# Serial steps of a recurrence wait for the next unit's tiled matmuls and share their groups

## Chip, cores and metric

One core of a Trainium2 chip runs the whole program. The metric is device time in microseconds (us), the median of several runs; lower is better. The engines are TensorE (PE, with PEld for its weight loads), VectorE (DVE), ScalarE (ACT), GpSimd (POOL) and SyncE (SP), which issues the DMA transfers.

## The reference

A decoder trunk of two layers, 512 positions, model width 1024, all in float32. Each layer projects its input x with one wide matrix into four gated branches of width 512, and merges them:

```
for l in range(2):
    h = x @ w_in[l]                      # split among the branches
    y_rwkv = rwkv7(...)                  # branch 0
    y_mla  = latent_attention(...)       # branch 1
    y_conv = conformer_conv(...)         # branch 2
    y_mem  = cross_attention(...)        # branch 3
    proj   = einsum('bsnc,ncd->bsnd', stack(y_rwkv, y_mla, y_conv, y_mem), w_o_branch[l])
    merged = sum(sigmoid(merge + b_gate[l]) * proj, over n)
    x = layer_norm(alpha * x + merged @ w_out[l])
```

The branch that the change touches is a recurrence over the positions, for 8 heads with a state of 64 x 64 each:

```
def step(state, inp):
    r_t, w_t, k_t, v_t, a_t, b_t = inp
    sa = einsum('bhvk,bhk->bhv', state, a_t)
    state = state * w_t + sa[..., None] * b_t + v_t[..., None] * k_t
    return state, einsum('bhvk,bhk->bhv', state, r_t)
y = group_norm(y) * lnx_g + lnx_b + bonus, then times silu(gate)
```

## The kernel before

**One stream and side tasks.** The large projections are matmuls of 128x128 weights by 512 columns, each product made of three (high by low, high by high, low by high parts), called from `mm3` through `MM` (L286). They form one stream in a fixed order (`stream`). Everything else (attention blocks, convolution, the recurrence) is written as Python generators, "tasks". A planner (`Plan`) decides once, while the program is built, where a task's next piece goes between pieces of the stream. It keeps its own clock per engine; a task that yields a function sleeps until it is true, one that yields "slack" waits for the planner's DVE clock, one that yields "small" has a piece of tiled 64x64 matmuls. The planner holds "small" pieces back (for up to `GATHER`) unless TensorE has just been switched to another tile shape, so that pieces that are due together come together. On the chip nothing of that is left but an order of instructions per engine and semaphore waits between engines.

**The recurrence in units.** `rwkv_unit` handles two channel blocks (four heads) over 256 positions: four units in each layer, `un` = 0 to 3, where units 1 and 3 go on from the state of 0 and 2. A unit works on four chunks of 64 positions with matrices of 64x64, as tiled matmuls of which four fit TensorE side by side. Its pieces are, by the names of the tiles that they write: zw (decay and rate), D (powers of the decay with a first column of ones), g (products of keys and receptances), M and Mc (the triangular part and its 16x16 diagonal blocks), a substitution on POOL that inverts those blocks (Mc goes out to a scratch tensor and comes back as W; the result comes back as zc, tc and zq, over SP's queue), bo and tk (full matmuls and transposes), x0, x1, x2 (the inverse is put together by blocks), va, gb (which gives Gs, H, B and Y0), then the **serial steps** w0 to w3: one after the other the state is multiplied by Gs (two tiled matmuls of 64x64 for each of two channel blocks) and S = w * D + H is formed on DVE. yb then applies the states to B, Y0 is added, eight bn_stats and bn_aggr and POOL's gr give the norm, ACT applies it to yb, ty transposes it and DVE adds it into r.

**What sets the order.** The units overlap: a unit starts when `L["mids"] == un` (the unit ahead has formed Gs, H, B, Y0). Its x0 waits until its substitution is back and `L["chains"] == un`, that is until the unit ahead has done all its serial steps and yb. The serial steps yield "small" and run as soon as the planner can place them. Tiles of a unit are in a pool (`rk`) by tags; tiles of one tag share a buffer, and T, Q, Z and PT are taken over by Gs, H, B and Y0. D has two buffers of its own, `dpads`, whose first column is set once at the start.

**After the last unit.** When `L["units"]` is 4 the recurrence's pool is closed, and the phase that ends the layer opens in the same memory: in layer 1 SP issues 16 loads of z and 8 of ln_g and ln_b, then the weights w220 and on. Weight loads have two buffers, so the load of w219 waits until the splits of w217 into high and low parts (ACT, then DVE) are done. ps_rg, ps_m and po are the gate, merge and output projections around that place.

Of the kernel before, what the change touches and what calls it, by code (L numbers as in the profile page):

```python
# [265 lines left out]
def trunk_kernel(ctx: ExitStack, tc: tile.TileContext, A, out, dbg=None):  # L266
# [4 lines left out]
    def MM(o, lhsT, rhs, start, stop, four=False):  # L271
        n = 1
        for d in rhs.shape[1:]:
            n *= d
        k, m = lhsT.shape[0], lhsT.shape[-1]
        plan.shape(64 if k <= 64 else 128, 64 if m <= 64 else 128)
        if max(k, m) <= 64:
            c = max(0.42 * n + 1.0, 29.0) if four else max(0.83 * n + 12.0, 59.0)
        elif rhs.dtype != F32 or n < 16:
            c = max(0.4167 * n + 13.0, 109.0) * (2 if rhs.dtype == F32 else 1)  # L280
        elif m <= 64:
            c = 0.83 * n + 3.0
        else:
            c = 1.667 * n + 5.0
        plan.op("PE", c, _names(o), _names(lhsT, rhs))
        plan.keep(nc.tensor.matmul(o, lhsT, rhs, start=start, stop=stop))  # L286

    def TR(o, i):
        plan.shape(128, 128)
        plan.op("PE", 109.0, _names(o), _names(i))  # L290
        plan.keep(nc.tensor.transpose(o, i, ident))  # L291
# [65 lines left out]
    for t in hpads:  # L357
        G.memset(t[:, 0:30], 0.0)
    dpads = [cp.tile([128, 8, 65], F32, tag=f"dpad{i}", name=f"dpad{i}") for i in range(2)]
    for t in dpads:  # L360
        G.memset(t[:, :, 0:1], 1.0)

# [235 lines left out]
    def layer_items(l):  # L598
# [97 lines left out]
        L["yr"] = [None] * 4  # L696
        L["units"] = L["chains"] = L["mids"] = L["subs"] = L["read"] = 0

# [13 lines left out]
        def chunks(ap):  # L712

            return ap.rearrange("p (a b) w -> p b a w", b=2)

        def by2(ap):
            return ap.rearrange("p (a b) w -> p a b w", a=2)

        def both(ap):

            return ap.rearrange("p s (c w) -> p (s c) w", w=64)

        def rwkv_unit(j0, hf, rkv):
# [8 lines left out]
            def rk(tag, shape, name=None, dt=F32, bufs=1):  # L732
                return L["rp"].tile([128] + shape, dt, tag=tag, name=(name or tag) + t, bufs=bufs)
# [19 lines left out]
            yield  # L753
            D = dpads[un % 2]
            S.activation(D[:, :, 1:65], both(cum), AF.Exp, scale=-1.0)
            E = rk("s0", [2, 256], "E")
            S.activation(E, cum, AF.Exp)
# [35 lines left out]
            V.reciprocal(rn[:, :, 1:4:2], s1[:, :, ::-1, 1])  # L793
            M = rk("M", [2, 4, 64])
            gm = g0[:, :, 0:256].rearrange("p h (s c w) -> p s h c w", s=2, c=2)
# [4 lines left out]
            M8 = M.rearrange("p s c w -> p (s c) w")  # L800
            Mc = rk("Mc", [8, 16])
            V.tensor_scalar(out=Mc, in0=M8[:, :, 0:16], scalar1=bm[:, 0:1], scalar2=None, op0=ALU.mult)
# [101 lines left out]

            yield lambda: L["subs"] > un and L["chains"] == un
            zc, tc_, zq = zt
# [8 lines left out]
            yield  # L915

            x0, y0 = yield from pg.take([128, 2, 512], "x0" + t, 2, "small")
            x0, y0 = (x.rearrange("p c (q s a w) -> p q s c a w", q=2, s=2, a=2) for x in (x0, y0))
# [52 lines left out]
            for s in SUB:  # L971
                for cp, c2, h in quads:
                    MM(x2[HALF[h ^ cp], 1, s, c2, h], NQ[s][HALF[c2], 2 * h + cp, 0], vt[s][HALF[c2], 2 * h + cp], start=True, stop=True, four=True)
            yield
            Z = rk("Z", [2, 4, 64], "Zi")
# [15 lines left out]
            pg.free()  # L991
            yield
            gbs = yield from pg.take([128, 2, 512], "gb" + t, 2, "small")
            gb, hh, y0 = ([x[:, :, a:b].rearrange("p c (a w) -> p c a w", a=2) for x in gbs] for a, b in ((0, 256), (256, 384), (384, 512)))
# [17 lines left out]
            yield  # L1012
            Gs, H, B, Y0 = (rk(tag, [2, 4, 64], n) for tag, n in (("T", "Gs"), ("Q", "H"), ("Z", "B"), ("PT", "Y0")))
            for s in SUB:
                V.tensor_tensor(out=by2(H[:, s]), in0=hh[s], in1=chunks(D[:, 4 * s:4 * s + 4, 64:65]).to_broadcast([128, 2, 2, 64]), op=ALU.mult)
                V.tensor_tensor(out=by2(Gs[:, s]), in0=gb[s][:, :, :, 0:64], in1=cc("id2")[:, 0:64].unsqueeze(1).unsqueeze(1).to_broadcast([128, 2, 2, 64]), op=ALU.add)
                S.copy(by2(Y0[:, s]), y0[s])
# [3 lines left out]
            L["mids"] += 1  # L1021
            yield


            states = [[zero, zero] if hf == 0 else [state[j] for s, j in js]]
            for c in range(4):
                e = 2 * (c % 2) + c // 2
                if hf == 0 and c == 0:
                    states.append([H[:, s, 0] for s in SUB])
                elif hf == 0 or c < 3:  # L1030
                    ps, = yield from pa.take([128, 2, 64], f"w{c}" + t, 1, "small")
                    for s in SUB:
                        for half in HALF:
                            MM(ps[half, s], Gs[half, s, e], states[c][s][half], start=True, stop=True)
                    yield
                    s1 = rk("S", [2, 64], f"S{c}", bufs=6)
                    for s in SUB:
                        V.scalar_tensor_tensor(out=s1[:, s], in0=ps[:, s], scalar=D[:, 4 * s + c, 64:65], in1=H[:, s, e], op0=ALU.mult, op1=ALU.add)
                    pa.free()
                    states.append([s1[:, s] for s in SUB])  # L1040
                    yield
            for s, j in js:
                state[j] = states[-1][s]
            ps, = yield from pg.take([128, 2, 512], "yb" + t, 1, "small")
            yp = ps[:, :, 0:256].rearrange("p h (s a w) -> p s h a w", s=2, a=2)
# [3 lines left out]
            yield  # L1049
            yb = rk("yb", [2, 4, 64])  # L1050
            for s in SUB:
# [8 lines left out]
            for e in range(8):  # L1060
                if e % 2 == 0:
                    yield "slack"
                V.bn_stats(bs[:, 6 * e:6 * e + 6], y8[:, e])
            yield "slack"
            for e in range(8):
# [12 lines left out]
            for a in range(4):  # L1078
                TR(ps[:, 128 * a:128 * a + 128], y8[:, 2 * a:2 * a + 2].rearrange("p e w -> p (e w)"))
            yield  # L1080
            for s, j in js:
                yield "slack"
                for a in range(2):
                    src = ps[:, 256 * s + 128 * a:256 * s + 128 * a + 128].rearrange("p (c w) -> p c w", c=2)
                    o = rr[s].rearrange("p (b a w) -> p b a w", b=2, a=2)[:, :, a]
                    if a:
                        src = src[:, ::-1]
                    V.scalar_tensor_tensor(out=o, in0=src, scalar=pr("lnx_g", j), in1=o, op0=ALU.mult, op1=ALU.add)
# [933 lines left out]
```

## Time and profile before

| | before |
|---|---|
| median of 3 runs | 1519.35 us (1518.24 to 1521.86) |
| span of the profiled execution | 1518.1 us |
| first matmul / last matmul's end in it | 6.1 us / 1508 us |
| TensorE busy | 1485.7 us |
| DVE, ACT, POOL busy | 1072.7, 686.6, 135.8 us |

How to read it: the span runs from the first to the last instruction of one execution. "Busy" counts from an instruction's start to its modelled end, and matmuls are pipelined, so the ends overlap the next starts; for TensorE the distance between starts says more than the duration. In a timeline row stand the start, the duration, engine, line, operation, the tiles written and read, the tile shape of the array (128*128 is full, 64*64 is tiled), the operand's size, and how many alike were merged in the row; in brackets the idle time before it and what ended it. A tiled float32 matmul shows as two records. In rows of groups stand the durations in ns (minimum, median, maximum).

### The profile page before, as it was taken

To read this page: it belongs to the slowest core of one execution; us is meant where nothing else is said; L and a number is where in the kernel's file an instruction comes from. 1 tells how busy PE (TensorE), PEld (TensorE's weight loads), DVE (VectorE), ACT (ScalarE), POOL (GpSimd) and SP (SyncE) were. 2 spreads that over 40 slices of the span, in tenths; PEclk is the share of its full clock that TensorE was granted. 3 is DMA by queue.
4 is the path that set the end of the run, shared out by engine and by line. 5 is a ranking of instruction groups with operands and counts; after the bars stand their busy time and mean duration, and the time that the engine had idled before them with its cause. 6 is when DMAs were issued, how large, how long until landed. Compare 5 with 4: busy or idle time off the path is not lost.

```text
span 1518.1 us, 29700 instructions
## 1 busy us (share of the span) xinstructions
PE 1485.7 (98%) x11896; PEld 1238.0 (82%) x11896; DVE 1072.7 (71%) x2231; ACT 686.6 (45%) x1499; POOL 135.8 (9%) x323
## 2 busy tenths in 40 slices
PE   8999999999999999999999999999999999999997
PEld 8877788887887878888999877888887878788886
DVE  5788988765757675555554889997766586756747
ACT  5535653445245453344255556533443545443432
POOL 0000000030402021000010000000030303120002
PEclk9999999999999999999999999999999999999999
DMA  6443333322232323433343252433232323235231
GB/s 211 124 113 93 104 100 98 98 85 83 74 93 60 94 74 93 139 98 114 123 146 114 81 125 69 121 107 97 81 99 61 93 64 93 69 95 181 98 116 65
DMA packets 89018, 153.54 MB, mean 101 GB/s; under 512 B 41008, under 2 KB 47152, under 8 KB 88880
## 3 DMA queue, kind: packets, MB, share of 16 engines
q1 hardware_dynamic: 88880, 151.65, 33.9%
q8 instruction: 93, 1.52, 0.4%
q14 instruction: 45, 0.37, 0.1%
HBM read 134.32 MB, written 5.77 MB: 92 GB/s over the span
## 4 chain that ended last, share of the span: by engine, by line
PE 89%; DVE 5%; DMA 2%; ACT 2%; issue 1%; SPq 1%; POOL 0%; ACTq 0%; DVEq 0%; POOLq 0%
PE ps_m L286 22%; PE po L286 11%; PE ps_cg L286 3%; PE ps_rg L286 3%; PE ps_v L286 3%; PE ps_xg L286 3%; PE ps_mg L286 3%; PE ps_k L286 3%; PE ps_r L286 3%; PE ps_val L286 3%; PE pz L286 2%; PE ms L286 2%; PE pl L286 2%; PE ps_glu L286 2%; PE ps_xq L286 2%; PE x L286 2%
## 5 line engine op out<-in xcount | busy, mean ns | idle before, releaser
L235 DVE SCALAR_TENSOR_TENSOR cacc<-hpad,prm,cacc 128x512 f32<-128x512 f32 x240 | 178.9, 748 | 3.3
L235 ACT ACTIVATE tm<-ps_m,prm 128x512 f32<-128x512 f32 x64 | 44.1, 689 | 148.5 <-PE ps_m L286 134.7
L235 DVE SCALAR_TENSOR_TENSOR mt<-tm,po 128x512 f32<-128x512 f32 x48 | 33.0, 687 | 79.2 <-PE po L286 79.1
L235 POOL TENSOR_SCALAR ZT<-W 64x256 f32<-64x256 f32 x8 | 4.8, 600 | 621.8 <-DMA W<-scr 287.7
L235 POOL TENSOR_TENSOR ZT<-ZT,tmpW 64x14 f32<-64x14 f32 (+6 forms) x112 | 44.0, 393 | 8.8
L235 ACT ACTIVATE mP<-ms,nmm 128x512 f32<-128x512 f32 (+3 forms) x64 | 33.7, 529 | 18.3 <-DVE nmm L235 17.4
L235 POOL TENSOR_TENSOR tmpW<-ZT,W 64x14 f32<-64x14 f32 (+6 forms) x112 | 39.9, 356 | 7.9
L235 ACT COPY mPT<-mt 128x512 f32<-128x512 f32 (+3 forms) x64 | 26.7, 429 | 22.4 <-PE mt L291 17.1
L235 DVE TENSOR_TENSOR merged<-merged,mt 128x512 f32<-128x512 f32 x48 | 33.8, 704 | 1.6
L235 DVE TENSOR_REDUCE nmm<-ms 128x1 f32<-128x512 f32 (+3 forms) x64 | 29.9, 483 | 0.6 <-PE ms L286 0.2
L235 POOL TENSOR_SCALAR gr<-gm 128x8 f32<-128x8 f32 x8 | 2.3, 286 | 311.2 <-DVE gm L235 311.2
L291 PE MATMUL mt<-cst,mP 128*128 128x128 f32 x160 | 27.1, 276 | 2.6 <-DVE mP L235 2.2
L235 DVE SCALAR_TENSOR_TENSOR merged<-tm,po 128x512 f32<-128x512 f32 x16 | 11.0, 687 | 22.0 <-PE po L286 20.3
L235 DVE TENSOR_SCALAR mP<-mP,smm 128x512 f32<-128x512 f32 (+3 forms) x64 | 24.8, 387 | 2.3
L235 ACT ACTIVATE yb<-yb,mr,gr 128x64 f32<-128x64 f32 x64 | 22.1, 430 | 9.0 <-DVE mr L235 9.0
L235 POOL TENSOR_SCALAR lrs<-lmv 128x1 f32<-128x1 f32 x8 | 2.5, 315 | 263.5 <-DVE lmv L235 261.8
L291 PEld LDWEIGHTS mt<-cst,mP 128*128 128x128 f32 x160 | 18.6, 141 | 8.2 <-ACT mo L235 2.2
L235 ACT ACTIVATE z<-z,lnb,lrs 128x256 f32<-128x256 f32 (+1 forms) x16 | 9.6, 647 | 31.2 <-DVE lnb L235 31.2
L286 PE MATMUL ms<-kTl,qT 96*128 96x512 f32 (+3 forms) x64 | 22.2, 347 | 0.0
L286 PE MATMUL mo<-mPT,v 128*64 128x128 f32 x320 | 21.4, 278 | 0.5 <-ACT mPT L235 0.5
L286 PE MATMUL ms<-kTh,qT 96*128 96x512 f32 (+3 forms) x64 | 20.6, 322 | 0.0
L286 PEld LDWEIGHTS mo<-mPT,v 128*64 128x64 f32 x320 | 17.3, 136 | 4.0 <-issue 2.9
(3535 smaller groups left out, 5323.2 us busy)
## 6 DMA issues: line engine op xcount, KB each, us to landing
w<-in_w_ch_dram SPq DMA_DIRECT2D x146, 512.0 KB, 3.6
w<-in_w_o_dram SPq DMA_DIRECT2D x32, 512.0 KB, 3.6
w<-in_w_out_dram SPq DMA_DIRECT2D x16, 512.0 KB, 3.6
w<-in_w_lat_dram SPq DMA_DIRECT2D x16, 336.0 KB, 3.3
w<-in_w_mk_dram SPq DMA_DIRECT2D x8, 512.0 KB, 3.5
w<-in_w_mv_dram SPq DMA_DIRECT2D x8, 512.0 KB, 3.5
w<-in_w_qk_dram SPq DMA_DIRECT2D x8, 320.0 KB, 3.1
x<-in_xT_dram SPq DMA_DIRECT2D x8, 256.0 KB, 5.6
```

What stands on the lines that cost most here:

```text
L235: return self.plan.keep(f(*a, **k))
L286: plan.keep(nc.tensor.matmul(o, lhsT, rhs, start=start, stop=stop))
L291: plan.keep(nc.tensor.transpose(o, i, ident))
```

## The change

- The serial steps get further waits in the planner: w0 and on wait until `L["chains"] == un` and until the next unit has reached its x0 (`L["fronts"] > un + 1`, not for unit 3); yb waits until the next unit has issued x2 (`L["backs"] > un + 1`).
- x0 of a unit no longer waits for the unit ahead to have finished its chain, but for the unit two ahead to have issued ty (`L["ends"] >= un - 1`); gb waits for `L["chains"] == un` instead.
- Gs, H, B and Y0 get tiles of their own, as they now live on while the next unit uses T, Q, Z and PT. yb takes tag T.
- D moves into the pool under tag M (so M is a cut of the same buffer), its first column is set in each unit, and its last columns, which H and S need later, are copied to dl. Mc goes under tag zc. S has four buffers instead of six.
- In unit 3 the bn_stats, bn_aggr and additions behind ty don't yield "slack" any more.

```diff
-    dpads = [cp.tile([128, 8, 65], F32, tag=f"dpad{i}", name=f"dpad{i}") for i in range(2)]
-    for t in dpads:
-        G.memset(t[:, :, 0:1], 1.0)
...
-            D = dpads[un % 2]
+            D = rk("M", [8, 65], "D")
+            G.memset(D[:, :, 0:1], 1.0)
             S.activation(D[:, :, 1:65], both(cum), AF.Exp, scale=-1.0)
+            dl = rk("dl", [8, 1], bufs=2)
+            S.copy(dl, D[:, :, 64:65])
...
-            M = rk("M", [2, 4, 64])
+            M = rk("M", [8, 65]).rearrange("p c w -> p (c w)")[:, 0:512].rearrange("p (s c w) -> p s c w", s=2, c=4)
...
-            Mc = rk("Mc", [8, 16])
+            Mc = rk("zc", [8, 16], "Mc")
...
-            yield lambda: L["subs"] > un and L["chains"] == un
+            yield lambda: L["subs"] > un and L["ends"] >= un - 1
...
+            L["fronts"] += 1
             x0, y0 = yield from pg.take([128, 2, 512], "x0" + t, 2, "small")
...
+            L["backs"] += 1
             yield
             Z = rk("Z", [2, 4, 64], "Zi")
...
+            yield lambda: L["chains"] == un
             gbs = yield from pg.take([128, 2, 512], "gb" + t, 2, "small")
...
-            Gs, H, B, Y0 = (rk(tag, [2, 4, 64], n) for tag, n in (("T", "Gs"), ("Q", "H"), ("Z", "B"), ("PT", "Y0")))
+            Gs, H, B, Y0 = (rk(tag, [2, 4, 64], n) for tag, n in ((n, n) for n in ("Gs", "H", "B", "Y0")))
...
             L["mids"] += 1
-            yield
-
+            yield lambda: L["chains"] == un and (un == 3 or L["fronts"] > un + 1)
...
-                    s1 = rk("S", [2, 64], f"S{c}", bufs=6)
+                    s1 = rk("S", [2, 64], f"S{c}", bufs=4)
                     for s in SUB:
-                        V.scalar_tensor_tensor(out=s1[:, s], in0=ps[:, s], scalar=D[:, 4 * s + c, 64:65], in1=H[:, s, e], op0=ALU.mult, op1=ALU.add)
+                        V.scalar_tensor_tensor(out=s1[:, s], in0=ps[:, s], scalar=dl[:, 4 * s + c], in1=H[:, s, e], op0=ALU.mult, op1=ALU.add)
...
+            yield lambda: un == 3 or L["backs"] > un + 1
             ps, = yield from pg.take([128, 2, 512], "yb" + t, 1, "small")
...
-            yb = rk("yb", [2, 4, 64])
+            yb = rk("T", [2, 4, 64], "yb")
...
-                if e % 2 == 0:
+                if e % 2 == 0 and un < 3:
                     yield "slack"
...
+            L["ends"] += 1
             yield
             for s, j in js:
-                yield "slack"
+                if un < 3:
+                    yield "slack"
```

More of the change, by code (lines that the diff above doesn't have):

```diff
@@ L696, in layer_items @@
         L["yr"] = [None] * 4
-        L["units"] = L["chains"] = L["mids"] = L["subs"] = L["read"] = 0
+        L["units"] = L["chains"] = L["mids"] = L["subs"] = L["read"] = L["fronts"] = L["backs"] = L["ends"] = 0
         quads = [(cp, c2, h) for cp in range(2) for c2 in range(2) for h in range(2)]
@@ L1012, in rwkv_unit @@
             yield
-            Gs, H, B, Y0 = (rk(tag, [2, 4, 64], n) for tag, n in (("T", "Gs"), ("Q", "H"), ("Z", "B"), ("PT", "Y0")))
+            Gs, H, B, Y0 = (rk(tag, [2, 4, 64], n) for tag, n in ((n, n) for n in ("Gs", "H", "B", "Y0")))
             for s in SUB:
-                V.tensor_tensor(out=by2(H[:, s]), in0=hh[s], in1=chunks(D[:, 4 * s:4 * s + 4, 64:65]).to_broadcast([128, 2, 2, 64]), op=ALU.mult)
+                V.tensor_tensor(out=by2(H[:, s]), in0=hh[s], in1=chunks(dl[:, 4 * s:4 * s + 4]).to_broadcast([128, 2, 2, 64]), op=ALU.mult)
                 V.tensor_tensor(out=by2(Gs[:, s]), in0=gb[s][:, :, :, 0:64], in1=cc("id2")[:, 0:64].unsqueeze(1).unsqueeze(1).to_broadcast([128, 2, 2, 64]), op=ALU.add)
@@ L1079, in rwkv_unit @@
                 TR(ps[:, 128 * a:128 * a + 128], y8[:, 2 * a:2 * a + 2].rearrange("p e w -> p (e w)"))
+            L["ends"] += 1
             yield
             for s, j in js:
-                yield "slack"
+                if un < 3:
+                    yield "slack"
                 for a in range(2):
```

## The prediction

> **What bounds the kernel now.** I read the page first, then the busy time by stages, the waits of TensorE in the recurrence's stages, and the timeline around single matmul groups.
>
> ```profile
> span 1518.1 us, 29700 instructions
> PE 1485.7 (98%) x11896; PEld 1238.0 (82%) x11896; DVE 1072.7 (71%) x2231; ACT 686.6 (45%) x1499; POOL 135.8 (9%) x323
> PEclk9999999999999999999999999999999999999999
> PE 89%; DVE 5%; DMA 2%; ACT 2%; issue 1%; SPq 1%; POOL 0%; ACTq 0%; DVEq 0%; POOLq 0%
> ```
>
> TensorE (PE) is busy 98% of the span at full granted clock, and 89% of the chain that ended last is its own work. The four recurrence units of each layer run in two stretches (columns: stretch, length, busy time of PE, PEld, DVE, ACT and POOL with counts, granted clock, DMA share, GB/s):
>
> ```profile
> 313.00:617.00 304.00, 301.95 (x3537) 244.66 (x3536) 199.82 (x437) 130.26 (x285) 55.05 (x138) 1.00 0.29 82
> 1089.00:1384.00 295.00, 293.92 (x3500) 237.26 (x3498) 199.87 (x443) 128.38 (x282) 57.50 (x138) 1.00 0.29 81
> 1508.00:1518.10 10.10, 0.00 (x0) 0.00 (x0) 5.93 (x14) 1.58 (x3) 3.26 (x5) 0.66 0.32 104
> ```
>
> In these 599 us TensorE lacks only 2.05 + 1.08 = 3.1 us. What it waited for there, first stretch and then second (total us, times, longest):
>
> ```profile
> PE x L286 <- DVE PT L235: 1.1, 2, 0.6
> PE ps_m L286 <- issue: 1.0, 1, 1.0
> ...
> PE gb L286 <- DVE VA L235: 0.3, 1, 0.3
> PE x L286 <- DVE PT L235: 0.3, 1, 0.3
> ```
>
> So a change of when things wait can win at most about 3 us here. A larger gain must shorten the stream of matmuls itself, and "busy" hides a part of that stream which is no work: the time around a change between full 128*128 matmuls and tiled 64*64 ones. The next rows show one serial step (w, eight records) between full matmuls:
>
> ```profile
> 373.40 0.39 PE L286 MATMUL ps_m<-xh,w59h 128*128 128x512 f32 x1
> 373.63 0.40 PE L286 MATMUL ps_m<-xh,w59l 128*128 128x512 f32 x1
> 373.96 0.45 PE L286 MATMUL w<-S,Gs 64*64 64x64 f32 x8
> 374.34 0.50 PE L286 MATMUL ps_m<-xl,w59h 128*128 128x512 f32 x1
> 374.67 0.39 PE L286 MATMUL ps_m<-xh,w59h 128*128 128x512 f32 x1
> ```
>
> Starts are what to read. Two full matmuls follow each other at 0.23 us (373.40 to 373.63). Into the tiled group it is 0.33, out of it the second full matmul follows the first at 0.33, and the first stands 0.38 after the group's start. From 373.63 to 374.67 are 1.04 us where two plain steps would take 0.46: the step costs the stream **0.58 us**, though its eight records, last started at 373.96 + 0.45 - 0.22 (one record's duration) = 374.19, are spaced 0.23 / 7 = 0.033 us.
>
> **The change, part by part.** *Fewer groups.* Three w steps and one yb step of each unit are tiled. Today each stands alone. The built order of the two programs (no time is in it) holds 9336 matmul instructions in both, all of the same kinds; the tiled 64*64 groups fall from 80 to 57. Units 0 to 2 of each layer have their w steps behind the next unit's x0, x1, x2 groups and their yb beside its va: 6 x 4 = 24, less one (the last w of layer 0's unit 1 still stands alone), so 17 w and 6 yb joins. Unit 3 has nobody to join.
>
> What a joined w still costs, from both sides: its own spacing, 8 x 0.033 = 0.26 us, or that of the four-tile groups, which is
>
> ```profile
> 512.64 0.69 PE L286 MATMUL x<-T,M 64*64 64x64 f32 x32
> 513.15 0.65 PE L286 MATMUL x<-M,T 64*64 64x64 f32 x32
> ```
>
> 0.51 / 32 = 0.016, so 0.13. I take 0.26, its own row: the saving is 0.58 - 0.26 = 0.32 us (0.45 at the other end). For yb:
>
> ```profile
> 539.87 0.39 PE L286 MATMUL ps_cg<-xh,w82l 128*128 128x512 f32 x1
> 540.19 0.27 PE L286 MATMUL yb<-zero,B 64*64 64x64 f32 x2
> ...
> 540.82 0.50 PE L286 MATMUL ps_cg<-xl,w82h 128*128 128x512 f32 x1
> 541.15 0.39 PE L286 MATMUL ps_cg<-xh,w82h 128*128 128x512 f32 x1
> ```
>
> From 539.87 to 541.15 are 1.28, less 0.46 plain: 0.82. Joined, 32 records at 0.016 are 0.50: again 0.32 saved. Sum: 23 x 0.32 = **7.4 us** less. If a join saved nothing (a change from four-tile x to two-tile w inside a group is not in this trace) it would be 0; with the thinner spacing 17 x 0.45 + 6 x 0.32 = 9.6.
>
> The Trainium skill, "TensorEngine Tiling (Array Packing)", section "Key Properties", says that changing the tiling mode drains TensorE and changing only the tile does not. By that rule the end at 0 falls away and the sum stays 7.4; the trace agrees where it can (steps of 0.33 at the change of mode, 0.016 from tile to tile inside x), and no run here yet shows x beside w.
>
> *New waits in the joined groups.* TensorE works in order, so a group now starts when the later of two operands is there, and everything queued behind it, the full matmuls first, waits too. The serial step's DVE work, and what x1 waits for:
>
> ```profile
> L235 DVE SCALAR_TENSOR_TENSOR S<-w,dpad,H x48: 256/277/285, 372.7 to 1379.3; 128x64 f32<-128x64 f32 x48
> L235 ACT COPY P<-x x16: 366/373/374, 353.0 to 1356.5; 128x256 f32<-128x256 f32 x16
> L235 DVE COPY PT<-x x16: 416/424/425, 354.5 to 1356.9; 128x256 f32<-128x256 f32 x16
> ```
>
> S is two operations of 0.28 us against the at least six full matmuls (1.4 us at 0.23) that the new order places between two groups. P and PT together are 2 x (0.37 + 0.42) = 1.6 us; they stand ahead of S on DVE, and the w behind x0 adds 0.26 us of cover to the same six matmuls. The two additions on yb (0.76 together in a row further down) come ahead of VA on DVE in the four groups where yb's matmuls stand ahead of va's, and those of va then run beside them:
>
> ```profile
> 522.80 1.10 PE L286 MATMUL va<-RA,Zi 64*64 64x128 f32 x32
> ```
>
> In the two groups with va first, VA is first on DVE as well. So I take 0 for the change in stalls; bounds: all of today's 1.7 us at PT and VA gone, or each of 23 groups late by half of the longest PT stall, 23 x 0.3 = 7 us more. The second is far, since the same distances today give 1.7 us over 80 groups; I put the likely top at 2.5.
>
> *Own tiles.* The memset of D's first column moves into each unit, and each unit copies the last columns of D to dl on ACT:
>
> ```profile
> L235 POOL MEMSET dpad<- x2: 112/112/112, 1.4 to 1.4; 128x8 f32 x2
> ...
> L235 ACT ACTIVATION_READ_ACCUMULATOR mP<-ms,nmm 128x1 f32 x64 | 12.6, 197 | 0.0
> ...
> L235 ACT ACTIVATE Q<-zq,cst x32: 385/388/402, 348.9 to 1350.3; 128x128 f32<-128x128 f32 x32
> ```
>
> Six memsets more are 0.7 us on POOL; eight copies of 128x8 lie between 0.20 and 0.39 us each, 1.6 to 3.1 us in all on ACT, which is 45% busy. dl is first read for H, behind gb; D's column is read by AR. Both have tens of matmuls of the other branches as cover; without it they would cost these sums once. The shared tags (D with M, Mc with zc, yb with T, four S instead of six) bring no reader that is not past by then in the new order: M's last reader is x0, T's is x2, and yb(n) is transposed well ahead of T of unit n + 2.
>
> *Queues that the step moves past.* Each unit's later steps, now 340 to 390 matmul instructions later, issue no DMA. On POOL they issue gr, which today can sit inside the next unit's substitution, waiting:
>
> ```profile
> 414.24 0.55 POOL L235 TENSOR_SCALAR gr<-gm 128x8 f32<-128x8 f32 x1 [1.27 <-DVE gm L235]
> 414.87 1.65 POOL L235 TENSOR_TENSOR gr<-gr,mhalf 128x8 f32<-128x8 f32 x1
> ```
>
> In the new order all substitutions run unbroken, so up to 1.27 + 0.55 + 1.65 = 3.5 us go from that chain in one unit. The next D memset may wait behind gr instead, its 0.55 + 1.65 = 2.2 us, with full matmuls running; worth 0 to the end.
>
> On SP, the phase behind the last unit begins with 24 loads (z, ln_g, ln_b) behind the load of w219, which waits for a split of w217 on DVE, which stands behind the last yb addition:
>
> ```profile
> 1381.07 0.76 DVE L235 TENSOR_TENSOR yb<-yb,Y 128x256 f32<-128x256 f32 x2 [0.92 <-PE yb L286]
> 1382.39 0.69 DVE L235 TENSOR_TENSOR w217l<-w,w217h 128x512 fp32r<-128x512 f32 x1 [0.57 <-ACT w217h L235]
> 1383.11 0.33 SPq L298 DMA_DIRECT2D w<-in_w_ch_dram  x1
> 1383.54 7.50 SPq L298 DMA_DIRECT2D z<-xtok  x16
> 1396.22 0.68 SPq L298 DMA_DIRECT2D w<-in_w_o_dram  x1
> 1398.54 0.39 PE L286 MATMUL ps_m<-xl,w218h 128*128 128x512 f32 x1
> 1403.74 0.62 ACT L235 CAST w220h<-w 128x512 fp32r<-128x512 f32 x1 [1.32 <-DMA w<-in_w_o_dram]
> 1404.40 0.69 DVE L235 TENSOR_TENSOR w220l<-w,w220h 128x512 fp32r<-128x512 f32 x1 [0.43 <-ACT w220h L235]
> 1409.42 0.39 PE L286 MATMUL po<-yrg0l,w220h 128*128 128x512 f32 x1
> ```
>
> Both programs run the same matmuls from the first ps_m behind the last unit (1398.54) on. The last yb matmul stands 79 instructions ahead of it before, 65 after, so the yb addition, the split, w219 and the burst come 14 x 0.23 = **3.2 us later** against that ps_m (2.6 if the split's own 0.57 us wait for ACT falls away). If the burst takes as long as it did, w220's low part is there at 1405.1 + 3.2 = 1408.3, ahead of po at 1409.4: 1.1 us of cover are left. I take 0.
>
> The rest of the stream, and the 10.1 us behind TensorE's last matmul, stay. **Sum**: the profiled execution 1518.1 - 7.4 = 1510.7. Its span is 1.25 us under the median of the runs (1519.35); the prediction for the median is 1510.7 + 1.25 = **1512.0**, own range 1510.0 (today's stalls gone, a little thinner w) to 1514.5 (2.5 more).
>
> **The rivals.** *New waits eat half.* The two operands of a joined group miss each other, each group 0.16 us late: 23 x 0.16 = 3.7, time 1515.7. For: three x groups today wait for PT, with 0.3 to 0.6. Against: w adds cover there.
>
> *It doesn't do what it says*: a join of x and w pays the change all the same. Then 1519.4. Against: nothing changes pace between x<-T,M and x<-M,T.
>
> *Slower: the burst behind the last unit.* Were DVE or ACT to hold the split of w217 (unit 3's bn_stats and the held yb of unit 2 now crowd there) by more than the 1.1 us of cover, po waits us for us. At 1.1 + 7.4 = 8.5 us beyond the 3.2 the gain is gone; at 13 the time is 1512.0 + 13 - 1.1 = 1523.9. For: ACT's eight yb activations and the yb additions stand ahead of the split. Against: in the new order they are about 3 us of work, not 9.
>
> *All stalls of the recurrence go as well*: 1512.0 - 1.7 = 1510.3.
>
> **How the numbers follow.** Forecast 0.72, all stalls gone 0.06, half eaten 0.12, no saving 0.04, burst 0.06. A measurement tells about 0.2% (3.0 us) from no change, so under 1516.3 counts as faster: 0.72 + 0.06 + 0.07 of the half case = 0.85. Within: the other 0.05 of that case, 0.04, and 0.01 of the burst = 0.10. Slower: 0.05. The range reaches from 1509.5 (a thinner w) to 1516.5, over the half case, and leaves out the last two.
>
> **What would show it.** Right: 57 tiled 64*64 groups; w's eight records beside x at a spacing near 0.03 us without a step of 0.33 between them; TensorE's span from first to last matmul shorter by about 7; lack of PE in the two stretches near 3 us. Wrong: waits of x, va or gb for S, PT or VA of over 3 us in all; po behind the last unit waiting for w220; a gap of 0.1 us between x and w in a group.

## The result, and the profile after

| | before | after |
|---|---|---|
| median (lowest to highest), first set | 1519.84 us (1518.24 to 1521.86), 4 runs | 1510.01 us (1507.76 to 1510.82), 4 runs |
| ratio | | 0.9931, 95% interval 0.9917 to 0.9944 |
| the same two kernels in a later set | 1520.84 us, 23 runs | 1510.41 us, 5 runs; ratio 0.9926 (0.9915 to 0.9938) |
| span of the first profiled execution | 1518.1 us | 1507.8 us |
| TensorE busy | 1485.7 us | 1475.7 us |
| tiled 64*64 groups | 80 | 57 |

The change makes the kernel 10 us faster, about 0.7%; 7.4 us were predicted. By the ratio the changed kernel stands at 0.9931 x 1519.35 = 1508.9 us, 0.6 us under the lower end of the range (1509.5); the plain median of its four runs, 1510.01 us, lies just above that end. The forecast had the direction and the mechanism; the gain was taken too small.

The page of the changed kernel, the lines that answer to those of before:

```profile
span 1507.8 us, 29728 instructions
PE 1475.7 (98%) x11896; PEld 1237.5 (82%) x11896; DVE 1072.6 (71%) x2231; ACT 688.1 (46%) x1507; POOL 134.3 (9%) x329
PEclk9999999999999999999999999999999999999999
PE 91%; DVE 4%; DMA 2%; ACT 2%; issue 1%; SPq 0%; POOL 0%; ACTq 0%; DVEq 0%; POOLq 0%
```

As many TensorE instructions as before, 10.0 us less of busy time, and TensorE is still what bounds the kernel: 98% busy, 91% of the chain that ended last. Eight more ACT instructions are dl's copies; their 1.5 us more of ACT time cost the end nothing.

The busy time by stages (columns as before: stretch, length, PE, PEld, DVE, ACT, POOL, granted clock, DMA share, GB/s), with the two recurrence stretches cut six and four us shorter because the program is through with them that much sooner, and then what TensorE waited for in each:

```profile
313.00:611.00 298.00, 297.57 (x3536) 244.28 (x3536) 197.96 (x432) 132.17 (x288) 57.59 (x141) 1.00 0.29 84
1083.00:1374.00 291.00, 288.91 (x3485) 237.12 (x3486) 195.18 (x426) 127.52 (x283) 53.08 (x141) 1.00 0.29 82
1497.70:1507.80 10.10, 0.00 (x0) 0.00 (x0) 6.02 (x14) 1.63 (x4) 3.33 (x5) 0.64 0.31 104
```

```profile
PE x L286 <- DVE PT L235: 0.4, 1, 0.4
...
PE zw L286 <- issue: 1.2, 1, 1.2
PE x L286 <- issue: 0.6, 1, 0.6
PE w L286 <- DVE S L235: 0.3, 1, 0.3
```

TensorE now lacks 0.43 + 2.09 = 2.5 us in the stretches, where it lacked 3.1. Waits for operands (PT, S) are 0.7 us of it, where PT and VA had 1.7; two stops of 1.2 and 0.6 us that belong to no operand are the rest. The 10.1 us behind the last matmul are what they were.

**Where the time went, by parts of the program.** The clearest reading of a change like this is the distance between the same two matmuls in both kernels. Four rows of the changed kernel's timeline set the borders: the first record of the first unit's g, and the first ps_m behind the last unit, in each layer.

```profile
313.14 0.34 PE L286 MATMUL g<-AR,bt 64*64 64x64 f32 x8
643.61 0.39 PE L286 MATMUL ps_m<-xl,w99h 128*128 128x512 f32 x1
1083.54 0.29 PE L286 MATMUL g<-AR,bt 64*64 64x64 f32 x4
1388.31 0.40 PE L286 MATMUL ps_m<-xl,w218h 128*128 128x512 f32 x1
```

So layer 0's recurrence part is 643.61 - 313.14 = 330.5 us long and layer 1's 304.8. The table gives these parts for every profile taken, each from the same four matmuls of its own timeline (us; the runs themselves are told below):

| profile | groups | up to first g | layer 0 | between | layer 1 | behind | layer 0 + 1 |
|---|---|---|---|---|---|---|---|
| before, three profiles | 80 | 313.4, 315.6, 313.1 | 336.5, 335.5, 336.2 | 440.0, 440.2, 440.1 | 308.7, 308.4, 308.7 | 119.6, 119.5, 119.5 | 645.2, 643.9, 645.0 |
| after, three profiles | 57 | 313.1, 311.8, 315.7 | 330.5, 330.4, 330.4 | 439.9, 439.9, 444.5 | 304.8, 304.2, 304.0 | 119.5, 119.5, 119.6 | 635.3, 634.6, 634.4 |
| own_tiles | 80 | 313.8 | 335.5 | 440.0 | 308.5 | 125.5 | 644.0 |
| own_slack | 80 | 312.4 | 335.2 | 439.8 | 308.4 | 119.5 | 643.7 |
| w_alone | 74 | 315.9 | 334.0 | 441.2 | 307.7 | 119.5 | 641.6 |
| slack3 | 57 | 312.6 | 330.3 | 439.4 | 308.3 | 121.2 | 638.7 |
| gather0 | 60 | 311.9 | 332.0 | 441.3 | 304.6 | 119.8 | 636.5 |
| gather2000 | 56 | 315.7 | 330.8 | 440.0 | 302.8 | 119.6 | 633.6 |
| gather2400 | 56 | 317.0 | 330.8 | 440.0 | 308.6 | 122.0 | 639.4 |

The whole gain lies in the two recurrence parts: their sum is 644.7 us on the mean of three profiles before and 634.7 after, **9.9 us less**. The other parts differ by as much between two profiles of one kernel as between kernels; why, the section on the hardware tells.

**The joined groups themselves.** First unit 0's x2, which nothing joins, in the changed kernel's timeline, with the full matmuls around it; then the next unit's x2 with a w step of unit 0 in its group:

```profile
358.99 0.39 PE L286 MATMUL ps_m<-xh,w57h 128*128 128x512 f32 x1
359.21 0.39 PE L286 MATMUL ps_m<-xh,w57l 128*128 128x512 f32 x1
359.53 0.69 PE L286 MATMUL x<-QQ,PP 64*64 64x64 f32 x32
360.05 0.65 PE L286 MATMUL x<-vt,NQ 64*64 64x64 f32 x32
360.62 0.50 PE L286 MATMUL po<-yxg0l,w58h 128*128 128x512 f32 x1
...
430.96 0.40 PE L286 MATMUL ps_k<-xh,w68l 128*128 128x512 f32 x1
431.28 0.38 PE L286 MATMUL w<-S,Gs 64*64 64x64 f32 x5
431.45 0.27 PE L286 MATMUL x<-QQ,PP 64*64 64x64 f32 x1
...
431.51 0.23 PE L286 MATMUL w<-S,Gs 64*64 64x64 f32 x2
431.56 0.58 PE L286 MATMUL x<-QQ,PP 64*64 64x64 f32 x28
...
432.60 0.50 PE L286 MATMUL ps_k<-xl,w68h 128*128 128x512 f32 x1
```

From the last full matmul ahead to the first one behind are 360.62 - 359.21 = 1.41 us alone and 432.60 - 430.96 = 1.64 with w: the step costs **0.23 us**. There is no step of 0.32 between w and x, only into and out of the group; records of w and x even alternate. Behind x0 it is less: the group of x0 alone lasts 1.943 us from its first record to its last, with w 2.115, so 0.17 us, the same in all six of them. A yb beside va costs 1.302 - 0.835 = 0.47 us (0.51 where va comes first). Alone, a w costs 0.58 and a yb 0.82, as before.

So each of the 6 w behind x0 saves 0.58 - 0.17 = 0.41 us, each of the 11 beside x1 or x2 0.58 - 0.23 = 0.35, and each of the 6 yb about 0.36: 2.5 + 3.9 + 2.2 = **8.5 us**, where the prediction had 23 x 0.32 = 7.4.

### The profile page after: what moved, and what is told of

Read it like the earlier page. It is cut to its first block, busy times and chain, and to the rows that moved or that the text cites. A ratio compares the mean times of both kernels' runs of the same rounds, so it can differ in the third digit from the quotient of the medians.

```text
span 1507.8 us, 29728 instructions
## 1 busy us (share of the span) xinstructions
PE 1475.7 (98%) x11896; PEld 1237.5 (82%) x11896; DVE 1072.6 (71%) x2231; ACT 688.1 (46%) x1507; POOL 134.3 (9%) x329
## 4 chain that ended last, share of the span: by engine, by line
PE 91%; DVE 4%; DMA 2%; ACT 2%; issue 1%; SPq 0%; POOL 0%; ACTq 0%; DVEq 0%; POOLq 0%
PE ps_m L286 23%; PE po L286 12%; PE ps_xg L286 3%; PE ps_cg L286 3%; PE ps_rg L286 3%; PE ps_k L286 3%; PE ps_mg L286 3%; PE ps_v L286 3%; PE ps_r L286 3%; PE ps_val L286 3%; PE ms L286 2%; PE pz L286 2%; PE ps_glu L286 2%; PE ps_xq L286 2%; PE pl L286 2%; PE x L286 2%
```

## The experiments

Each was timed against the kernel before on the same chip, in two sets of four kernels; the three runs of the last experiment have one time and one profile each.

**1. The changed kernel once more.** No edit.

> The changed kernel once more, unaltered, for its time on the chip of this set and for what repeats of its profile. Theory J (the joined groups are the gain: 17 w joins at about 0.37 us and 6 yb joins at about 0.36, 8.5 us, and the waits for operands that went from 2.6 to 0.9 us come with the new order): 9 to 11 us under the kernel before, ratio near 0.9933; waits of TensorE for PT, S and VA again 0.9 us within 0.2, at the same places (x1 of the first unit, w2 of the second layer's third unit). Theory P (the part of the gain beyond the predicted 7.4 us is the luck of one execution): waits at other places, and a gain nearer to 7.4, ratio 0.995. The stops that the profile puts to issue (1.5 and 0.8 us) belong to no operand: if they are the program's they recur at the same matmuls, if not they move.

1510.41 us, ratio 0.9926 (0.9915 to 0.9938). The waits for PT (0.4 us, x1 of the first unit) and S (0.3 us, w2 of layer 1's second unit, in the group of the third unit's x2) are at the same places; zw is stopped again, by 1.1 us. The second stop, of 0.6 us at an x, shrank to 0.1 us. So what goes beyond the 7.4 us is no luck of one execution.

**2. Own tiles, but no joining.** The two waits of the serial steps go; yb takes Gs's tag instead of T's, since T is in use at that time, and gb waits until the unit ahead is through with its last reads.

```diff
-            yield lambda: L["chains"] == un
+            yield lambda: L["ends"] >= un
             gbs = yield from pg.take([128, 2, 512], "gb" + t, 2, "small")
...
-            yield lambda: L["chains"] == un and (un == 3 or L["fronts"] > un + 1)
+            yield
...
-            yield lambda: un == 3 or L["backs"] > un + 1
...
-            yb = rk("T", [2, 4, 64], "yb")
+            yb = rk("Gs", [2, 4, 64], "yb")
```

> The changed kernel without the two waits of the serial steps, so that they stand alone as before: 80 tiled 64*64 groups, at the positions of before within 15 instructions; all the rest of the change stays (own tiles, dl, D in M's slot, four S, no slack in unit 3). Theory J: the gain is gone, 1518 to 1519.5 us, ratio 0.999 to 1.000; lone w steps cost 0.58 us as before. Theory O (own tiles, the relief of POOL's memsets and the unit without slack give what lies beyond the predicted 7.4 us): 1.5 to 2.5 us faster than before, ratio near 0.9985. If own tiles cost something by ACT's copies it would be slower than before, by up to 3 us.

1524.99 us, ratio 1.0024 (1.0013 to 1.0035): 3.7 us slower than before, which no theory had in full (the last had up to 3 us, by ACT's copies). The table shows where: the recurrence parts stand at 644.0 us, as before, so the joining is what the gain rests on; but behind the last unit 6 us are lost. The timeline there, ACT's, DVE's and SP's rows and then TensorE's, and the busy time of seven us of it:

```profile
1384.01 0.69 ACT L235 ACTIVATE tm<-ps_m,prm 128x512 f32<-128x512 f32 x1 [5.07 <-PE ps_m L286]
1388.15 0.69 DVE L235 TENSOR_TENSOR w217l<-w,w217h 128x512 fp32r<-128x512 f32 x1
1389.24 8.49 SPq L298 DMA_DIRECT2D z<-xtok  x16
1402.14 0.33 SPq L298 DMA_DIRECT2D w<-in_w_o_dram  x1
1410.22 0.50 PE L286 MATMUL po<-yrg0l,w220h 128*128 128x512 f32 x1 [1.34 <-ACT w220h L235]
1412.13 0.79 PE L286 MATMUL po<-yrg0h,w220l 128*128 128x512 f32 x1 [1.17 <-DVE w220l L235]
1412.72 0.63 PE L286 MATMUL po<-yrg1l,w220h 128*128 128x512 f32 x1
1413.14 0.63 PE L286 MATMUL po<-yrg1h,w220h 128*128 128x512 f32 x1
```

```profile
1410.00:1417.00 7.00, 5.60 (x14) 4.11 (x15) 4.98 (x12) 1.83 (x4) 0.00 (x0) 0.61 0.38 129
```

ACT stands 5.07 us at tm, which waits for a matmul; the split of w217 comes late behind it, the burst of loads behind that, and w220 is asked for 4.3 us after the first ps_m (1397.84). po then stands for both halves of w220, 2.5 us, and behind that the clock is granted at 0.61: full matmuls start 0.42 us apart (1412.72 to 1413.14) instead of 0.23 until 1418, which is another 3 us. This is the prediction's slower rival, "the burst behind the last unit", in a variant of the kernel.

**3. The same with the last unit's slack as before.**

```diff
-                if e % 2 == 0 and un < 3:
+                if e % 2 == 0:
                     yield "slack"
...
-            if un < 3:
-                yield "slack"
+            yield "slack"
...
-                if un < 3:
-                    yield "slack"
+                yield "slack"
```

> The changed kernel without both waits of the serial steps and with the slack yields of the last unit as before: 80 groups, each step alone, and only the own tiles (dl, D in M's slot, four S, no fixed pads) left of the change. The kernel without the waits alone (own_tiles) lost 5.9 us behind the last unit: po stood 1.5 and 1.3 us for the two halves of w220, whose load was issued 4.3 us behind the first ps_m, and the next fifteen matmuls then started 0.43 us apart instead of 0.23. Theory B (the missing slack put the end of the last unit ahead of the splits, and the burst of loads behind them came late): that loss goes, po does not wait, and the time is 1518 to 1520 us, 5 to 6 us under own_tiles. Theory O (own tiles cost it): still 1524 to 1525. If own tiles by themselves win something (waits for PT went from 1.1 and 0.3 us to one of 0.5), it stands 0.5 to 1.5 us under the kernel before.

1519.01 us, ratio 0.9995 (0.9987 to 1.0004): by the ratios 0.0029 x 1520 = 4.4 us under experiment 2, and 6.0 us in the part behind the last unit, which is back at 119.5 us. po waits for nothing there. The order on ACT tells why: here its last cast for the split of w217 stands ahead of tm (1379.03 and 1381.98 us), in experiment 2 behind it (1384.59 and 1384.01). So without the joining the missing slack is what brings the burst late, and **own tiles, dl, D in M's slot and four S together are worth nothing that can be told**.

**4. Only yb joins.**

```diff
-            yield lambda: L["chains"] == un and (un == 3 or L["fronts"] > un + 1)
+            yield
```

> The changed kernel without the first of the two waits alone: the w steps of units 0 to 2 go at once, by themselves, as before; yb still goes beside va. 74 groups. Theory J with the sizes read from the trace (a w join is worth 0.41 us beside x0 and 0.35 beside x1 and x2: 17 joins 6.3 us; a yb join 0.36): about 6.3 us slower than the changed kernel, 2.2 us faster than before, near 1517, ratio 0.9985. With the sizes of the prediction (0.32 each): 5.4 us slower than the changed kernel. If the waits for operands depend on the joins, some 1 us more on top.

1517.02 us, ratio 0.9977 (0.9968 to 0.9986), 6.6 us over the changed kernel (expected 6.3; 5.4 with the prediction's sizes). In the parts: 641.6 against 634.7, 6.9 us for the 17 w joins; and 643.8 (mean of own_tiles and own_slack) less 641.6, 2.2 us for the 6 yb joins. Both agree with the sizes read off the groups.

**5. The changed kernel with the last unit's slack put back**: the diff of experiment 3 upon the changed kernel.

> The changed kernel with the slack yields of the last unit put back, as units 0 to 2 have them. 57 groups at the same positions as the changed kernel. Theory J: no difference from the changed kernel, within 0.5 us. Theory O (the last unit's end without slack gives part of the gain, by an earlier split of w217 and an earlier burst of loads behind it): 1 us or more slower, with po waiting or the matmuls behind the last unit later.

1513.64 us, ratio 0.9954 (0.9941 to 0.9967): 3.2 us slower, so theory O's direction, by another path than it named. What TensorE waited for, and the timeline:

```profile
PE ty L291 <- ACT yb L235: 3.4, 4, 2.4
```

```profile
1387.71 2.76 ACT L235 ACTIVATE yb<-yb,mr,gr 128x64 f32<-128x64 f32 x8 [0.83 <-DVE mr L235]
1388.54 0.33 PE L291 MATMUL ty<-cst,yb 128*128 128x128 f32 x1 [2.35 <-ACT yb L235]
1389.20 0.33 PE L291 MATMUL ty<-cst,yb 128*128 128x128 f32 x1 [0.34 <-ACT yb L235]
```

With slack between its pieces the last unit's group norm is so late that ty waits 3.4 us for it. po doesn't wait. Without these 3.4 us the recurrence parts are 638.7 - 3.4 = 635.3 us, as in the changed kernel, so the joins save as much here. But with the slack kept on both sides (this run and experiment 3) only 0.9995 - 0.9954, about 6.2 us, of the 10 reach the end: the measured gain needs both edits. The condition `un < 3` is thus worth 3 us with the joining and costs 4 to 6 us without it.

**6. More and less gathering ahead of a tiled group.** One constant of the planner: how long, by its own clock, a small task waits for company after the last tiled group.

```diff
-GATHER = 1500.0
+GATHER = 2000.0
```

> The changed kernel with 2000 ns in place of 1500 ns for what the order gathers ahead of a tiled group: 56 groups, the lone w2 of layer 0's second unit joined as well, and three to five more full matmuls between the groups of x. The last yb stands 16 matmuls later (8767 instead of 8751). Theory J: one more join 0.35 us and waits for S and PT of 0.4 to 0.8 us gone, about 1 us under the changed kernel, 1509.5. Theory B (the cover behind the last unit is down to 0.5 us in the changed kernel, and 16 matmuls later is 3.7 us): po waits 2 to 3 us for w220, and the clock goes down behind that wait for 2 to 3 us more: 1514 to 1516.

1509.82 us, ratio 0.9932 (0.9917 to 0.9946): no difference from the changed kernel that can be told. The recurrence parts are 1.1 us shorter (633.6), as theory J expected; that profile's first part, 315.7 us, is as long as the longest of the changed kernel (311.8 to 315.7), and the runs show no gain. po doesn't wait, though the last yb stands 16 matmuls later: theory B's step from yb's position to the burst doesn't hold: the burst begins 14.2 us ahead of the first ps_m, 10.4 in the changed kernel.

With 0 in place of 1500:

> The changed kernel with nothing gathered ahead of a tiled group: 60 groups, all 18 w joins and two of the six yb joins left. Theory J: four yb joins fewer at 0.36 us, less one w join more at 0.35: 1.1 us slower than the changed kernel. Theory W (the order by which operands are late decides, with fewer full matmuls between the groups of layer 0): waits of x1 for PT and of w for S grow by 0.3 us or more in several groups, 2 to 4 us slower. Theory B: last yb 10 matmuls later, po waits 1 to 2 us and the clock goes down behind it.

1514.50 us, ratio 0.9961 (0.9948 to 0.9975), by the ratios 4.6 to 5.3 us over the changed kernel, more than theories J and W allow. The recurrence parts are 1.8 us longer (expected: 1.1 for the joins, and more by the waits, of which va for RA came to 0.7 us and x for PT to 0.7 in place of 0.4). po doesn't wait. The profile taken is that of the fastest of the five runs (1511.29). Part of the rest is the clock: the five runs have a mean granted clock of 0.994 on the median, the nine of the changed kernel 0.996, and at equal clock gather0 is 0.9 us slower (0.996) to 3.6 us slower (0.994). Why its clock is lower isn't known; this result is only explained in part.

With 2400:

> The changed kernel with 2400 ns gathered: 56 groups, but in layer 1's second unit x0, w1 and x1 stand in one group with no full matmul between, and w3 goes with va; the last yb stands 37 matmuls later than in the changed kernel. Theory W: x1 there waits for P and PT, 1.6 to 2.5 us. Theory B: po waits for w220 up to 8 us and the clock goes down for some 3 us behind that: 1515 to 1523. Theory J alone: 0.4 us under the changed kernel.

1518.08 us, ratio 0.9990 (0.9980 to 1.0000). The time is within theory B's range, but its cause is another: po doesn't wait. The last unit's group norm comes late, as in experiment 5:

```profile
1394.24 0.33 PE L291 MATMUL ty<-cst,yb 128*128 128x128 f32 x1 [2.87 <-ACT yb L235]
```

and the clock is down behind it. x1, with no full matmul ahead of it, waited 0.7 us for PT, less than theory W's 1.6 to 2.5. No version beat the changed kernel by more than can be measured.

**7. Two more profiles of the kernel before, one more of the changed one.**

> The kernel before, unaltered, for a second profile: which of its waits in the two recurrence stretches are the program's. Theory T (the own tiles end them): x1 of layer 0's last unit waits for PT again by 0.6 us, x1 of layer 1's second unit by 0.3, gb for VA by 0.3; both stretches together again 1.5 us longer than in own_slack (643.7 us). Theory L (luck of one execution): they are elsewhere or half as long, and the stretches come to 643.5 to 644.5 us. The stop put to issue at the ps_m behind gb (1.0 us, the 3389th matmul) recurs in both cases, since two kernels of other tiles have it there too.

> The same once more, as for the run ahead of it: three profiles of the kernel before give a spread.

> The changed kernel, a third profile: the two recurrence stretches together 634.5 to 635.3 us as in the first two; x1 of the first unit waits for PT 0.4 us, w2 of layer 1's third unit for S 0.3, zw is stopped 1.1 to 1.3 us at the 8592nd matmul without an operand missing. Its span differs from the other two only where the granted clock dips.

1520.90, 1519.46 and 1515.85 us. The waits of x for PT in the kernel before come to 1.3, 0.9 and 2.0 us in its three profiles: the same three places, with sizes that change from one execution to the next. In own_tiles and own_slack only the first of the places is left, with 0.4 us, which speaks for theory T; but va then waits for RA, and bo, and 644.0 and 643.7 us are not below the spread of before (643.9 to 645.2) by enough to call it a gain. So the places belong to the program, and what own tiles are worth there isn't settled. The stop at matmul 3389 (counted from 0) recurs, with 1.0, 0.5 and 0.3 us. The third profile of the changed kernel has its recurrence parts at 634.4 us and its named waits as expected (PT 0.4, S 0.3; zw 1.0, a little under what was put down), though its span is 1514.1 us, for the reason in the section on the hardware.

## Why the prediction was off

- **Fewer groups** (23 joins): right, in number and in kind. Without them nothing is left of the gain (experiment 3), and w and yb joins come to 6.9 and 2.2 us of the parts.
- **What a join saves** (0.32 us, 7.4 in all): too small, the first term that was mis-sized. The step that failed is the price of a joined w, "its own row", 8 x 0.033 = 0.26 us. Measured are 0.17 and 0.23: the spacing of lone w records isn't theirs in company, they alternate with four-tile records and cost 21 to 28 ns each. The price lay between the two ends that the prediction had worked out (0.13 and 0.26); taking the upper one is most of the 1.1 us by which the joins were taken too small. yb's price (0.50) was right within 0.03.
- **By the Trainium skill**, "TensorEngine Tiling (Array Packing)", section "Key Properties", a change of tile alone doesn't drain TensorE; the trace agrees: no step between w and x, 0.09 and 0.11 us beyond a plain 0.23 into and behind the group. The rival "it doesn't do what it says" falls.
- **New waits in the joined groups** (0, bounds -1.7 to +7): the second mis-sized term. Counting every start in the two parts that comes over 0.15 us later than its neighbours' usual spacing, what operands held up came to 2.5, 2.1 and 3.2 us in the three profiles before and to 0.9 in each of those after: 1.7 us less, the very end that the prediction had put down as a bound and, added to its forecast, as a rival with a chance of 0.06. Not all of it is the new order: by the same count own_tiles and own_slack, where nothing joins, have 1.5 and 1.6 us. Stops without an operand went the other way, from 1.4, 0.6 and 0.4 to 2.2, 1.6 and 1.4, which the prediction didn't see. Net 0.8 us less. "New waits eat half" falls.
- **The sum.** 8.5 + 0.8 = 9.3 of the 9.9 us by which the parts are shorter; 0.6 are spread over steps too small to name. The two lower ends were never added in full: a thinner w (9.6 us) alone gives 1519.35 - 9.6 = 1509.75, stalls gone (1.7) as well 1508.05, and the range ends at 1509.5. Both came in part and at once.
- **Own tiles** (0): right; experiment 3.
- **The burst behind the last unit** (3.2 us later, 1.1 us of cover left, taken as 0): its outcome right, its margin nearly used up. The rows of the changed kernel:

```profile
1376.44 0.68 DVE L235 TENSOR_TENSOR w217l<-w,w217h 128x512 fp32r<-128x512 f32 x1
1377.88 7.45 SPq L298 DMA_DIRECT2D z<-xtok  x16
1390.63 0.49 SPq L298 DMA_DIRECT2D w<-in_w_o_dram  x1
1398.43 0.69 DVE L235 TENSOR_TENSOR w220l<-w,w220h 128x512 fp32r<-128x512 f32 x1
1399.22 0.39 PE L286 MATMUL po<-yrg0l,w220h 128*128 128x512 f32 x1
1399.67 0.39 PE L286 MATMUL po<-yrg0h,w220l 128*128 128x512 f32 x1
```

  The burst begins 1388.31 - 1377.88 = 10.4 us ahead of the first ps_m, where it began 1398.54 - 1383.54 = 15.0 ahead: 4.6 us later, not 3.2. w220's low part is ready at 1399.12, 0.10 us ahead of the first po by the prediction's measure (1.1 was left), 0.55 ahead of the matmul that reads it. The price of that rival was too low: it counted one us for each us of waiting, while experiment 2 paid 6 us for a wait of 2.5. And a step of it failed: it tied the split to the place of the last yb. Experiment 2's last yb came earlier than before's (matmul 8722 against 8737) and its burst 6.4 us later; experiment 3 has yb at the same place as experiment 2, and its burst begins 15.1 us ahead of the first ps_m instead of 8.6. What differs is what stands ahead of the split on ACT and DVE.
- **A part not costed at all**: the last unit without slack, which the prediction met only as a crowd on DVE. It decides 3 us with the joining and 4 to 6 without, in opposite directions.

## What to carry to other kernels

On an engine that is 98% busy, look for time inside "busy": a change between full and tiled matmuls cost 0.3 to 0.4 us each time around a group, and putting small tiled steps into groups that are there anyway won it back without removing an instruction. Price what joins by bounds from both rows, its own and that of the group it will stand in (here the truth lay between), and where two bounds can both come true, let the range hold their sum. And look at the end of the moved work: a piece that comes later there can push a weight split behind another engine's wait, and the load behind it.

## What the runs showed of the hardware

**A short wait can cost more than its length in clock.** The table's first and middle parts differ by up to 4.6 us between profiles of the same kernel. The granted clock tells it: in the third profile of the changed kernel

```profile
120.00:130.00 10.00, 9.07 (x34) 7.63 (x35) 7.32 (x21) 4.64 (x16) 0.00 (x0) 0.66 0.91 186
890.00:910.00 20.00, 17.68 (x74) 14.33 (x73) 13.16 (x29) 7.91 (x22) 0.00 (x0) 0.74 0.51 130
```

and in the first one in the same stretches

```profile
120.00:130.00 10.00, 8.80 (x52) 7.04 (x53) 8.81 (x26) 5.48 (x19) 0.00 (x0) 1.00 0.93 212
890.00:910.00 20.00, 17.88 (x110) 14.10 (x108) 18.70 (x47) 12.92 (x36) 0.00 (x0) 1.00 0.43 113
```

The busy time is alike, but 34 and 74 matmuls got through instead of 52 and 110. The missing clock is 0.34 x 10 = 3.4 and 0.26 x 20 = 5.2 us at most; the parts in which it lies are 2.5 and 4.6 us longer than in the first profile. All seventeen such dips in the thirteen profiles, the first and last ten microseconds aside, stood at a wait of TensorE of 1.3 to 2.9 us, and such waits had a dip in some executions and not in others: the wait of 1.7 us at pmv is in all thirteen profiles, a dip behind it in one (w_alone, where the middle part is 1.2 us longer). Every run has its mean granted clock on record, and the time goes with it: of the 23 runs of the kernel before in the later of the two sets, the four at 0.997 took 1517.7 to 1518.9 us and the five at 0.994 took 1521.0 to 1522.7. So much of the 3 us by which runs of one kernel differ is this. The Trainium skill, "TensorE: Matmul & The Clock Gate", section "HAM oscillation — how this bites in real kernels", warns of gaps over about 3.4 us. The measurement differs: in w_alone the one wait of 1.7 us at pmv was enough, in experiment 2 two of 1.34 and 1.17 us close together.

**Stops that belong to a place in the instruction stream.** zw's stop falls on matmul 8592 of the execution, counted from 0 over the trace's records, with no operand missing:

```profile
1142.31 0.39 PE L286 MATMUL zw<-lxw,lhw 128*128 128x256 f32 x1 [1.25 <-issue]
```

In ten of the thirteen profiles there is such a stop at matmul 8592, 8593 or 8594, whatever that matmul is: zw in seven besides the first, a ps_v in the first profile of before (0.2 us), a gb in gather2400 (0.7); two profiles of before and gather2000 have none. Matmul 3389 is such a place in the three profiles of before, in own_tiles and own_slack (a ps_m) and in gather2400 (a gb). The traces point at the loading of TensorE's instructions, which come by DMA:

```profile
q8 instruction: 93, 1.52, 0.4%
```

These are 93 packets of 16 KB, one each 16 us on the mean and one for about 11896 / 93 = 128 matmuls. By the times that the traces hold of single packets, each of the sixteen stops at the two places ends 1.2 to 1.5 us behind the recorded end of such a packet, and so do the three others of more than 0.15 us put to issue between 20 and 1500 us, the one at an x among them. Both places lie in or right behind the gb of a unit, 160 records that start within 2.75 us: more than a packet's worth of matmuls, where a packet lasts 16 us on the mean. That TensorE ran out of instructions there fits all of this; no run changed the loading to test it.
